# Diagonal blocks copied on chip instead of loaded twice, six loads moved to another queue, and two groups of tiles shifted by 64 bytes

## The chip, the core and the metric

The kernel runs on one core of a Trainium2 chip. A core has five engines that run side by side, each with its own queue of instructions that it works off in order: TensorE (PE, matrix products, with its weight loads listed apart as PEld), VectorE (DVE), ScalarE (ACT), GpSimd (POOL) and SyncE (SP), which here only issues transfers. ACT can issue transfers too; its other work then waits while it does. The transfers themselves run on 16 DMA engines. On-chip memory (SBUF) has 128 partitions; matrix products land in PSUM.

The metric is the device time of one execution in microseconds (us), as a median of several runs.

## The reference, cut to what matters

Two layers of a sequence encoder work on 256 positions of 1024 channels in float32. Each layer mixes positions by a retention branch and by a gated delta rule in both directions, merges the two with gates, and then applies a feed-forward block.

```python
for l in range(DEPTH):                       # 2 layers
    h = rmsnorm(x, norm1_g[l])
    (r_q, r_k, r_v, r_g, d_q, d_k, d_v, d_z, d_b, d_a, gate_raw) = split_cols(h @ w_in[l])
    y_ret = ...                              # retention, normed, times silu(r_g)
    od = gated_delta_bidir(dq, dk, dv, beta_f, beta_b, g_f, g_b)
    y_dn = ...                               # od normed, times silu(d_z)
    merged = gates[:, :, 0] * (y_ret @ w_proj_ret[l]) + gates[:, :, 1] * (y_dn @ w_proj_dn[l])
    x = x + merged @ w_out[l]
    h2 = rmsnorm(x, norm2_g[l])
    x = x + jnp.square(jax.nn.relu(h2 @ w_ff1[l])) @ w_ff2[l]
return rmsnorm(x, final_g)
```

The delta rule works in chunks of 128 positions. In each chunk, head and direction it solves a unit triangular system:

```python
a_mat = bc[..., :, None] * jnp.einsum('bhnid,bhnjd->bhnij', kc, kc) * dec_strict
lhs = a_mat + jnp.eye(CHUNK, dtype=jnp.float32)
sol = lax.linalg.triangular_solve(lhs, rhs, left_side=True, lower=True, unit_diagonal=True)
```

There are 8 heads, 2 chunks and 2 directions, which is 32 triangles of 128 x 128 in each layer.

## The kernel before

**Dense products.** Every weight matrix is read from HBM once. `tok_chunk` (L185) and `chan_pair` (L203) load raw tiles of 512 KB through SP's queue (L191, L209; tile names wraw and wrawc, three buffers), ACT makes a rounded high part (L181, whi), DVE the low remainder (L182, wlo), and PE adds three products of high and low parts (L198 to L200, or L216 to L218). The accumulators are named after their use: pcd are the delta inputs, padz and pcga the gates, pcpr and pcpd the two projections, pawo the output projection, pcf and paf the two feed-forward products. In `chan_pair` a row of weights is the stationary operand and 256 positions stream past; in `tok_chunk` the activations are stationary and 512 columns of weights stream.

**The triangular systems.** `delta_kk` (L435) forms the matrices, and `delta_solve` (L469) inverts all their 32 x 32 diagonal blocks at once on DVE into X (L482 to L488), copies the transposed inverses to XT (L490) and stores both to HBM as xd and xtd (L492, L493). `delta_levels` (L496) then builds the inverse of each 128 x 128 matrix from these blocks, for two halves of four heads (hf 0 and 1). Three tiles take the blocks from HBM, in pieces of 32 partitions x 8 matrices x 32 columns (32 KB each):

- dd (L514, L515), 8 loads: plane 0 and plane 1 hold the diagonal blocks of the direction b % 2, and of the other direction, as the products ps_y (L527) and ps_mt (L544) stream them;
- D64 (L520, named D in the profile), 4 loads: diagonal blocks in the left or right half of 64 columns;
- DTt (L522, named DT), 8 loads: the diagonal blocks of the transposed inverses; the rest of each tile is zeroed first by GpSimd (L517).

That is 20 loads for each half, 40 in a layer, all issued by SP. Four of the eight DTt blocks and two of the four D64 blocks of a half hold the same numbers as a block of dd on the same partitions. The steps that follow are small products in float32: ps_y, then W is rewritten (L530 on DVE, L532 on ACT), then ps_m (L537) fills D64 (L539), ps_mt fills the off-diagonal DT blocks (L547, L549), and two more products with 64 columns (L558, L568) finish the inverse. ps_y and ps_mt stream 32 columns past 128 x 128 weights.

**Order.** The two halves are generators that `drive` steps in turn. Which instruction an engine gets next is fixed before the run by a scheduler with a simulated clock: of those whose inputs it expects to be ready, the one that stands earlier in the program is put first, and loads and conversions of raw weights are moved 45 places ahead (WPRI). So dense work that stands later in the program fills PE's time while the small products wait. The gate product pcga and then the retention projection pcpr are the dense work behind `delta_levels`; the program's text has the small loads before the loads of pcpr's weights, and SP's queue holds them in that order. The DTt tiles of the second half share memory with X and XT, so their zeroing waits for the stores xd and xtd to end.

**Memory.** Tiles come from pools, one slot size for all users of a tag, slots one after the other. mTh and mTl, the high and low part of the merged branches and the stationary operands of pawo, use the two slots of tag E, which earlier hold the decay matrices E (L324). fh and fl, eight tiles each, are the stationary operands of paf; their pool lies at the start of a region that in layer 1 begins with the small pool fin (L826).

Of the kernel before, what the change touches and what calls it, by code (L numbers as in the profile page):

```python
# [9 lines left out]
F32R = mybir.dt.float32r  # L10
# [4 lines left out]
P = 128  # L15
D = 1024
S = 256
# [18 lines left out]
def tile_trunk(ctx, tc, x, norm1_g, w_in, conv_w, a_log, dt_bias, ret_gn_g, dn_norm_g,  # L36
               w_proj_ret, w_proj_dn, w_out, norm2_g, w_ff1, w_ff2, final_g, consts, out):
    nc = tc.nc
    DQ = nc.sync
    V, A, G, T = nc.vector, nc.scalar, nc.gpsimd, nc.tensor  # L40

    def pool(name, bufs, space=None, c=ctx):
        kw = {} if space is None else {"space": space}
        return c.enter_context(tc.tile_pool(name=name, bufs=bufs, **kw))
# [181 lines left out]
    for l in range(DEPTH):  # L226
        mctx = ctx.enter_context(ExitStack())
        mx = pool(f"mx{l}", 1, None, mctx)
        dl = pool(f"dl{l}", 1, None, mctx)
# [201 lines left out]
        blk = [slice(32 * b, 32 * b + 32) for b in range(4)]  # L431
# [64 lines left out]
        def delta_levels(hf, q):  # L496

            Av = q["Av"]
            D64 = D64h[hf]
            xv, xtv = (t[64 * hf:64 * hf + 64].rearrange("(d u b) (a e) -> d b a u e", d=2, b=4, e=32)  # L500
                       for t in (sc["xd"], sc["xtd"]))
            Dv = (xtv, xv)
            DTv = (xv, xtv)
            W = sc["W"][hf]
            dd = dl.tile([P, 2, 8, 32], F32, tag="dd", name="dd", bufs=2)
            if hf == 0:
                DTt = [hp.tile([P, 8, P], F32, tag=f"x{d}", name=f"DT{d}") for d in range(2)]
            else:
                DTt = [dl.tile([P, 8, P], F32, tag="GX"[d], name=f"DT{d}") for d in range(2)]
            G.memset(D64, 0.0)  # L510
            for b in range(4):

                d = b % 2
                DQ.dma_start(dd[blk[b], 0], Dv[d][d, b])  # L514
                DQ.dma_start(dd[blk[b], 1], DTv[1 - d][1 - d, b])  # L515
            for d in range(2):
                G.memset(DTt[d], 0.0)  # L517
                for e in range(2):
                    b = 2 * d + e
                    DQ.dma_start(D64[blk[b], :, 32 * e:32 * e + 32], Dv[d][d, b])  # L520
                for b in range(4):
                    DQ.dma_start(DTt[d][blk[b], :, blk[b]], DTv[d][d, b])  # L522
            yield

            ps = dps.tile([P, 8, 32], F32, tag="dps", name="ps_y")
            for u in range(8):
                T.matmul(ps[:, u, :], lhsT=W[:, u, :], rhs=dd[:, 0, u, :], start=True, stop=True)  # L527
            for d, b, c in PAIRS:
                if d:
                    V.tensor_copy(W[blk[c], :, blk[b]], ps[blk[c]])  # L530
                else:
                    A.activation(W[blk[c], :, blk[b]], ps[blk[c]], AF.Copy)  # L532
            yield
            for d, b, c in ((0, 0, 1), (1, 3, 2)):
                pm = dps.tile([P, 512], F32, tag="dps", name="ps_m")
                for u in range(8):
                    T.matmul(pm[:32, 32 * u:32 * u + 32], lhsT=DTt[d][:, u, blk[c]], rhs=W[:, u, blk[b]],  # L537
                             start=True, stop=True)
                V.tensor_scalar(D64[blk[c], :, 32 * (b % 2):32 * (b % 2) + 32],  # L539
                                pm[:32, :256].rearrange("p (u c) -> p u c", u=8), -1.0, None, ALU.mult)  # L540
            yield
            ps = dps.tile([P, 8, 32], F32, tag="dps", name="ps_mt")
            for u in range(8):
                T.matmul(ps[:, u, :], lhsT=W[:, u, :], rhs=dd[:, 1, u, :], start=True, stop=True)  # L544
            for d, b, c in PAIRS:
                if d:
                    V.tensor_scalar(DTt[d][blk[b], :, blk[c]], ps[blk[b]], -1.0, None, ALU.mult)  # L547
                else:
                    A.activation(DTt[d][blk[b], :, blk[c]], ps[blk[b]], AF.Copy, scale=-1.0)  # L549
            half = (slice(0, 64), slice(64, 128))  # L550
            yield

            Y6 = dl.tile([P, 8, 64], F32, tag="dd", name="Y6", bufs=2)
            for d in range(2):
                ss, oo = half[d], half[1 - d]
                ps = dps.tile([P, 8, 64], F32, tag="dps", name="ps_y6")
                for u in range(8):
                    T.matmul(ps[:64, u, :], lhsT=Av[d][ss, u, oo], rhs=D64[ss, u, :], start=True, stop=True)  # L558
                if d:
                    V.tensor_copy(Y6[oo], ps[:64])  # L560
                else:
                    A.activation(Y6[oo], ps[:64], AF.Copy)
            yield
            for d in range(2):
                ss, oo = half[d], half[1 - d]
                ps = dps.tile([P, 8, 64], F32, tag="dps", name="ps_m6")
                for u in range(8):
                    T.matmul(ps[:64, u, :], lhsT=Y6[oo, u, :], rhs=DTt[d][oo, u, oo], start=True, stop=True)  # L568
                if d:
                    V.tensor_scalar(DTt[d][ss, :, oo], ps[:64], -1.0, None, ALU.mult)  # L570
                else:
                    A.activation(DTt[d][ss, :, oo], ps[:64], AF.Copy, scale=-1.0)
            q.update(DT=DTt)
# [162 lines left out]
        def delta():  # L736
            qs = []
            for hf in range(2):
                q = yield from half_inputs(hf)
                delta_kk(hf, q)  # L740
                qs.append(q)
            delta_solve()
            yield
            drive(*(delta_levels(hf, qs[hf]) for hf in range(2)))
            for hf in range(2):
                yield from half_v(hf, qs[hf])
            yield
            drive(*(delta_out(hf, qs[hf]) for hf in range(2)))
# [28 lines left out]
        def gate(off, dst, nm):  # L777

            for i in range(4):
                ps = chan_pair(wl_[:, off + 256 * i:off + 256 * (i + 1)], hT_hi, hT_lo, nm)  # L780
                for e in range(2):
                    t_ = dst[i // 2][:, 2 * (i % 2) + e, :]
                    A.activation(t_, ps[e], AF.Tanh, scale=0.5)

        mT = [mx.tile([P, 4, S], F32, tag=f"sg{j}", name=f"mT{j}") for j in range(2)]
# [12 lines left out]
               lambda k: gT2[:, 32 + l:33 + l], yTh, yTl, "yd")  # L798
        tB = [dl.tile([P, 4, S], F32, tag=t, name="tB" + t, bufs=2) for t in ("ktok", "kq0")]
        gate(O_GB, tB, "gb")  # L800
        mTh, mTl = (dl.tile([P, 2, 4, S], F32R, tag="E", name="mT" + n, bufs=2) for n in "hl")
        mTh, mTl = ([m[:, j] for j in range(2)] for m in (mTh, mTl))
        for i in range(4):
            ps = chan_pair(w_proj_dn[l][:, 256 * i:256 * (i + 1)], yTh, yTl, "pd")
            for e in range(2):
                k = 2 * (i % 2) + e
# [21 lines left out]
        ff = pool(f"ff{l}", 1, None, fctx)  # L828
# [2 lines left out]
        r2 = rms("2", xh)  # L831
        rr2 = sm.tile([P, NT], F32, tag="rr2", name="rr2")
        V.tensor_tensor(rr2, r2, r2, ALU.mult)
        fh = [ff.tile([P, 4, S], F32R, tag=f"fh{i}", name=f"fh{i}") for i in range(8)]
        fl = [ff.tile([P, 4, S], F32R, tag=f"fl{i}", name=f"fl{i}") for i in range(8)]
        for i in range(16):
            ps = chan_pair(w_ff1[l][:, 256 * i:256 * (i + 1)], hT_hi, hT_lo, "f1")
            for e in range(2):
                k = 2 * i + e
# [20 lines left out]
        if last:  # L860

            r = fin.tile([P, NT], F32, tag="fr", name="fr")
            o = fin.tile([P, NT, D], F32, tag="o", name="o")
# [57 lines left out]
```

## Time and profile before

| | us |
|---|---|
| runs | 1119.09, 1125.75, 1119.31 |
| median of the runs | 1119.31 |
| the profiled execution | 1122.8 |
| its span | 1121.1 |
| mean granted TensorE clock | 0.974 |

The profiled execution ran 3.5 us longer than the median; 1.7 us of its time lie outside its span. The page of the profile gives each engine's busy time and share of the span, and then rows with the span cut in 40 slices of 28 us, each digit a share in tenths. The row PEclk shows the TensorE clock that was granted in a slice. Matmuls are pipelined, so their durations overlap: the pace of a series is read from the distance of their starts. A row of the timeline gives start, duration, engine, line, operation, the tile written and the tiles read, the count of merged instructions, and in brackets the idle time before it and what ended that. SPq and ACTq rows are the issue of a transfer, not its run.

### The profile page before, as it was taken

Reading aid. Unit: us, or ns where it says so; the run is one execution under the profiler, and the core shown is the slowest. Engines: PE = TensorE matmul, PEld = TensorE weight load, DVE = VectorE, ACT = ScalarE, POOL = GpSimd, SP = SyncE. Lnnn points to the kernel's source line nnn. Section 1 sums busy time; section 2 is a strip of 40 time slices with the busy share of each in tenths; the row PEclk is TensorE's granted clock in tenths of the full one; section 3 lists DMA queues with packets and bytes.
Section 4 is the critical chain, followed back from the end, with each engine's and each line's share of the span. In section 5 each row is a group of like instructions: output and inputs, shape, how many; then the busy total and the mean of one; then the engine's idle time right before and its main releaser. Section 6 shows DMA issues by size and latency. Waiting matters only on the chain.

```text
span 1121.1 us, 19644 instructions
## 1 busy us (share of the span) xinstructions
PE 1077.8 (96%) x7564; PEld 998.3 (89%) x7564; DVE 761.1 (68%) x1375; ACT 594.9 (53%) x1030; POOL 217.5 (19%) x237
## 2 busy tenths in 40 slices
PE   6989999999999999999979899999999999999997
PEld 5989888989999899988879888889999999999885
DVE  4879989735676676644469799895465766766453
ACT  5986555523354566533369765454333546665342
POOL 3076210100012043300020952000000111332000
PEclk9999999969999999999999999999699999999999
DMA  6575665553545566556556646656435465665563
GB/s 213 160 202 148 188 189 157 148 138 114 151 129 174 169 202 184 185 187 207 176 166 178 183 149 170 187 151 140 139 108 151 143 203 165 204 188 187 190 190 111
DMA packets 175760, 188.44 MB, mean 168 GB/s; under 512 B 36240, under 2 KB 137010, under 8 KB 175666
## 3 DMA queue, kind: packets, MB, share of 16 engines
q1 hardware_dynamic: 174288, 185.17, 55.5%
q10 hardware_dynamic: 1378, 2.02, 0.5%
q8 instruction: 59, 0.97, 0.4%
q14 instruction: 35, 0.29, 0.1%
HBM read 181.85 MB, written 5.31 MB: 167 GB/s over the span
## 4 chain that ended last, share of the span: by engine, by line
PE 41%; POOL 3%; DVE 3%; SPq 1%; DMA 1%; issue 1%; ACT 1%; POOLq 0%
PE pcf L218 3%; PE pcf L216 3%; PE pcf L217 3%; PE paf L200 3%; PE paf L198 3%; PE paf L199 3%; POOL E L335 3%; PE pcd L216 1%; PE pcd L217 1%; PE pcd L218 1%; DVE wlo L182 1%; PE pcpr L217 1%; PE pcpr L216 1%; PE pcpr L218 1%; PE parg L199 1%; PE pcpd L218 1%
## 5 line engine op out<-in xcount | busy, mean ns | idle before, releaser
L182 DVE TENSOR_TENSOR wlo<-wrawc,whi 128x1024 fp32r<-128x1024 f32 x192 | 238.1, 1241 | 111.9 <-ACT whi L181 110.6
L181 ACT ACTIVATE whi<-wrawc 128x1024 fp32r<-128x1024 f32 x192 | 202.4, 1057 | 141.6 <-PE pcpr L217 22.1
L181 ACT ACTIVATE whi<-wraw 128x1024 fp32r<-128x1024 f32 x128 | 135.6, 1059 | 183.2 <-PE paf L200 91.5
L182 DVE TENSOR_TENSOR wlo<-wraw,whi 128x1024 fp32r<-128x1024 f32 x128 | 156.7, 1227 | 109.1 <-ACT whi L181 109.1
L217 PE MATMUL pcf<-h2l,whi 128*128 128x256 f32 x512 | 142.4, 281 | 0.0
L218 PE MATMUL pcf<-h2h,wlo 128*128 128x256 f32 x512 | 141.6, 281 | 0.0
L216 PE MATMUL pcf<-h2h,whi 128*128 128x256 f32 x512 | 140.8, 282 | 0.0
L216 PE MATMUL pcd<-hTh,whi 128*128 128x256 f32 x384 | 111.3, 294 | 2.4 <-DVE rw L662 2.4
L217 PE MATMUL pcd<-hTl,whi 128*128 128x256 f32 x384 | 109.9, 287 | 0.0
L218 PE MATMUL pcd<-hTh,wlo 128*128 128x256 f32 x384 | 108.5, 288 | 0.0
L199 PE MATMUL paf<-wlo,fh 128*128 128x512 f32 x256 | 100.7, 393 | 0.0
L200 PE MATMUL paf<-whi,fl 128*128 128x512 f32 x256 | 100.7, 393 | 0.0
L217 PEld LDWEIGHTS pcf<-h2l,whi 128*128 128x128 f32 x512 | 98.0, 191 | 0.0
L218 PEld LDWEIGHTS pcf<-h2h,wlo 128*128 128x128 f32 x512 | 95.9, 188 | 0.0
L216 PEld LDWEIGHTS pcf<-h2h,whi 128*128 128x128 f32 x512 | 95.0, 188 | 0.0
L198 PE MATMUL paf<-whi,fh 128*128 128x512 f32 x256 | 90.5, 393 | 0.0
L843 POOL TENSOR_TENSOR fz<-fz 128x256 f32<-128x256 f32 x64 | 68.3, 1068 | 112.0 <-ACT fz L842 94.8
L216 PEld LDWEIGHTS pcd<-hTh,whi 128*128 128x128 f32 x384 | 74.5, 195 | 4.2 <-issue 2.5
L335 POOL TENSOR_SCALAR E<-E,gx 128x128 f32<-128x128 f32 x64 | 58.9, 940 | 95.9 <-DMA E<-rowd 50.1
L217 PEld LDWEIGHTS pcd<-hTl,whi 128*128 128x128 f32 x384 | 74.5, 194 | 0.5
L218 PEld LDWEIGHTS pcd<-hTh,wlo 128*128 128x128 f32 x384 | 73.5, 194 | 0.6 <-DVE wlo L182 0.3
L364 DVE SCALAR_TENSOR_TENSOR cacc<-pcd,cw,cacc 128x255 f32<-128x255 f32 (+1 forms) x144 | 67.3, 477 | 6.2 <-ACT cac L360 5.1
(266 smaller groups left out, 2644.3 us busy)
## 6 DMA issues: line engine op xcount, KB each, us to landing
wrawc<-in_w_in_dram SPq DMA_DIRECT2D x96, 512.0 KB, 3.9
wrawc<-in_w_ff_dram SPq DMA_DIRECT2D x64, 512.0 KB, 3.8
wraw<-in_w_ff_dram SPq DMA_DIRECT2D x64, 512.0 KB, 3.6
wraw<-in_w_in_dram SPq DMA_DIRECT2D x48, 512.0 KB, 3.7
wrawc<-in_w_proj_ret_dram SPq DMA_DIRECT2D x16, 512.0 KB, 3.7
wrawc<-in_w_proj_dn_dram SPq DMA_DIRECT2D x16, 512.0 KB, 3.4
wraw<-in_w_out_dram SPq DMA_DIRECT2D x16, 512.0 KB, 3.8
E<-rowd SPq DMA_DIRECT2D x16, 256.0 KB, 5.6
```

The costliest lines, as they stand in the source:

```text
L181: A.activation(hv, raw, AF.Copy)
L182: V.tensor_tensor(lv, raw, hv.bitcast(F32), ALU.subtract)
L198: T.matmul(ps[t], lhsT=a, rhs=wh[:, kk, :], start=k == 0, stop=False)
L199: T.matmul(ps[t], lhsT=a, rhs=wl[:, kk, :], start=False, stop=False)
L200: T.matmul(ps[t], lhsT=b, rhs=wh[:, kk, :], start=False, stop=k == nk - 1)
L216: T.matmul(ps[i], lhsT=wh[:, kk, c], rhs=a, start=k == 0, stop=False)
L217: T.matmul(ps[i], lhsT=wh[:, kk, c], rhs=b, start=False, stop=False)
L218: T.matmul(ps[i], lhsT=wl[:, kk, c], rhs=a, start=False, stop=k == KT - 1)
L335: G.tensor_scalar(E[:, c, h, :], E[:, c, h, :], gc[:, c, u:u + 1], 0.0, ALU.subtract, ALU.min)
L364: V.scalar_tensor_tensor(a[:, o], ps[i][:, q], wk(k), a[:, o], ALU.mult, ALU.add)
L843: G.tensor_tensor(z2, z, z, ALU.mult)
```

## The change

It touches four places.

1. In `delta_levels`, both DTt tiles are zeroed ahead of the loads.
2. Of the eight DTt blocks, the four with d != b % 2 are copied by GpSimd from plane 1 of dd; of the four D64 blocks, the two with d == e are copied from plane 0. These 12 copies in a layer are of 32 partitions x 256 numbers and take the place of 12 loads.
3. The other four DTt loads and two D64 loads of a half are issued by SP in the first half and by ACT in the second (`q_`). The eight dd loads of each half stay with SP. In a layer SP now issues 22 small loads and ACT 6.
4. mTh now starts 64 bytes into its slot; mTl starts at the beginning of its slot, and as each slot of the tag has become 64 bytes longer, the second slot begins 64 bytes later. In layer 0 the tile fh0 begins 64 bytes into its slot, which is longer by as much, so that all tiles of that pool behind it are shifted too. In layer 1 that pool is as before.

```diff
             G.memset(D64, 0.0)
+            for d in range(2):
+                G.memset(DTt[d], 0.0)
+            q_ = (DQ, nc.scalar)[hf]
             for b in range(4):
 
                 d = b % 2
                 DQ.dma_start(dd[blk[b], 0], Dv[d][d, b])
                 DQ.dma_start(dd[blk[b], 1], DTv[1 - d][1 - d, b])
-            for d in range(2):
-                G.memset(DTt[d], 0.0)
-                for e in range(2):
-                    b = 2 * d + e
-                    DQ.dma_start(D64[blk[b], :, 32 * e:32 * e + 32], Dv[d][d, b])
-                for b in range(4):
-                    DQ.dma_start(DTt[d][blk[b], :, blk[b]], DTv[d][d, b])
+
+            for d, b in ((0, 1), (1, 2), (0, 0), (0, 2), (1, 1), (1, 3), (0, 3), (1, 0)):
+                if d != b % 2:
+                    G.tensor_copy(DTt[d][blk[b], :, blk[b]], dd[blk[b], 1])
+                else:
+                    q_.dma_start(DTt[d][blk[b], :, blk[b]], DTv[d][d, b])
+            for b in range(4):
+                d, e = b // 2, b % 2
+                to = D64[blk[b], :, 32 * e:32 * e + 32]
+                if d == e:
+                    G.tensor_copy(to, dd[blk[b], 0])
+                else:
+                    q_.dma_start(to, Dv[d][d, b])
             yield
...
-        mTh, mTl = (dl.tile([P, 2, 4, S], F32R, tag="E", name="mT" + n, bufs=2) for n in "hl")
+        mTh, mTl = (dl.tile([P, 16 + 8 * S], F32R, tag="E", name="mT" + n, bufs=2)[:, o:o + 8 * S]
+                    .rearrange("p (j k s) -> p j k s", j=2, k=4) for n, o in (("h", 16), ("l", 0)))
...
-        fh = [ff.tile([P, 4, S], F32R, tag=f"fh{i}", name=f"fh{i}") for i in range(8)]
+
+        lead = 16 if l == 0 else 0
+        fh = [ff.tile([P, lead * (i == 0) + 4 * S], F32R, tag=f"fh{i}", name=f"fh{i}")[:, lead * (i == 0):]
+              .rearrange("p (k s) -> p k s", k=4) for i in range(8)]
```

## The prediction

> **What bounds the kernel now.** I read the page's busy shares first, then its clock row, then TensorE's waits, then a table of windows laid on the half-clock stretches.
>
> ```profile
> span 1121.1 us, 19644 instructions
> PE 1077.8 (96%) x7564; PEld 998.3 (89%) x7564; DVE 761.1 (68%) x1375; ACT 594.9 (53%) x1030; POOL 217.5 (19%) x237
> PEclk9999999969999999999999999999699999999999
> PE ps_y L527 <- DMA dd<-xd: 3.2, 2, 2.2
> ```
>
> TensorE (PE) is busy 96% of the span, so only two things can pay: time in which it stands, and time in which it runs slowly. The wait that this change touches is small, 3.2 us in two pieces (one in each layer). What follows it is larger:
>
> ```profile
> 225.47:228.88 3.41, 1.24 (x12) 1.07 (x10) 0.00 (x0) 0.38 (x1) 0.00 (x0) 1.00 0.42 67
> 228.88:245.95 17.07, 16.54 (x124) 16.18 (x124) 7.78 (x13) 5.30 (x9) 0.00 (x0) 0.50 0.63 177
> 587.28:590.69 3.41, 1.90 (x17) 1.70 (x16) 1.79 (x7) 2.57 (x5) 0.00 (x0) 1.00 0.82 253
> 655.55:658.96 3.41, 2.10 (x15) 1.92 (x16) 3.28 (x9) 1.06 (x1) 0.93 (x2) 1.00 0.45 147
> 778.43:781.84 3.41, 2.33 (x26) 2.12 (x25) 0.00 (x0) 0.50 (x2) 0.00 (x0) 1.00 0.41 66
> 781.84:805.73 23.89, 22.83 (x174) 21.85 (x172) 9.69 (x15) 6.83 (x11) 0.00 (x0) 0.50 0.48 143
> ```
>
> Columns: stretch, length, busy time of PE, weight loads, DVE, ACT and POOL, then granted clock, DMA share, GB/s. Right behind the stall the granted clock is 0.50 for 17.07 us in layer 0 and for 23.89 us in layer 1. A stretch with 1.90 us or 2.10 us of PE work (587.28, 655.55) keeps the clock at 1.00 beyond it; the one at 778.43 holds more, 2.33 us, and loses it. The difference is the kind of work, seen in PE's timeline:
>
> ```profile
> 226.05 0.28 PE L218 MATMUL pcga<-hTh,wlo 128*128 128x256 f32 x1
> 228.50 3.24 PE L527 MATMUL ps_y<-dd,W 128*128 128x32 f32 x16 [2.17 <-DMA dd<-xd]
> 236.13 7.04 PE L544 MATMUL ps_mt<-dd,W 128*128 128x32 f32 x32
> 243.77 0.41 PE L217 MATMUL pcpr<-yrl,whi 128*128 128x256 f32 x1
> 243.98 0.41 PE L218 MATMUL pcpr<-yrh,wlo 128*128 128x256 f32 x1
> 246.29 0.28 PE L217 MATMUL pcpr<-yrl,whi 128*128 128x256 f32 x1
> 246.40 0.28 PE L218 MATMUL pcpr<-yrh,wlo 128*128 128x256 f32 x1
> 779.74 1.94 PE L527 MATMUL ps_y<-dd,W 128*128 128x32 f32 x16 [1.08 <-DMA dd<-xd]
> 781.62 0.93 PE L537 MATMUL ps_m<-W,DT 128*32 128x32 f32 x16
> 783.05 2.12 PE L537 MATMUL ps_m<-W,DT 128*32 128x32 f32 x32 [0.51 <-DVE D L539]
> 786.66 7.04 PE L544 MATMUL ps_mt<-dd,W 128*128 128x32 f32 x32
> 793.51 0.56 PE L216 MATMUL pcpr<-yrh,whi 128*128 128x256 f32 x1
> 797.20 3.31 PE L558 MATMUL ps_y<-D,A 64*64 64x64 f32 x32
> 808.92 1.90 PE L568 MATMUL ps_m<-DT,Y 64*64 64x64 f32 x32
> ```
>
> When the dense gate work (pcga) ends at 226.33, PE has only thin matmuls, 32 columns wide, and no dense work to mix in. Dense work (pcpr) begins at 242.98 in layer 0 and at 793.51 in layer 1. At half clock pcpr matmuls start 0.21 us apart (243.77, 243.98), at full clock 0.11 to 0.12 (246.29, 246.40; I use 0.117). Why no dense work: the pcpr weights stand behind the small loads on SP's queue.
>
> ```profile
> 211.94 0.33 SPq L514 DMA_DIRECT2D dd<-xd  x1
> 220.27 3.16 SPq L522 DMA_DIRECT2D DT<-xtd  x4
> 226.92 0.45 SPq L515 DMA_DIRECT2D dd<-xd  x1
> 233.39 23.41 SPq L209 DMA_DIRECT2D wrawc<-in_w_proj_ret_dram  x8
> 764.22 0.33 SPq L514 DMA_DIRECT2D dd<-xd  x1
> 778.19 0.45 SPq L515 DMA_DIRECT2D dd<-xd  x1
> 784.65 26.74 SPq L209 DMA_DIRECT2D wrawc<-in_w_proj_ret_dram  x8
> ```
>
> Forty small loads fill the queue from 211.94 to 233.39 (21.45 us, 0.54 each) and from 764.22 to 784.65 (20.43 us).
>
> **The change, part by part.** *Loads removed or moved.* Of 20 loads in each half, 6 become copies; in the second half 6 more go to ACT. SP keeps 8+6 and 8, which is 22 of 40. At the same price each SP needs 11.8 us in layer 0 and 11.2 us in layer 1: the first pcpr weight is issued near 223.7 (9.7 us earlier) and near 775.5 (9.2 us earlier). The last dd load, whose landing ended PE's wait 1.6 us after its issue (226.92 to 228.50), would land by about 225 and 777, before pcga ends. So the waits of 2.17 and 1.08 us go. What is late next is PE's own thin chain and its evacuations (the 0.5 us idle before ps_m).
>
> *The stretch at full clock.* One thin group of 16 ps_y takes 1.88 us (779.74 to 781.62). I price ps_mt, of the same shape, equally, though no row shows it at full clock: 3.76 us for both halves. Four ps_m groups at 0.93 are 3.72, three gaps of 0.51 are 1.53. Sum 10.9 us, against 16.65 in layer 0 (226.33 to 242.98) and 14.84 in layer 1 (778.67 to 793.51): 5.7 and 3.9 us saved. Behind it, 14 pcpr matmuls of layer 0 at 0.21 and not 0.117 cost 1.3 us; in layer 1 33 of them cost 3.2 us, and two ps_y groups about 2.0 (3.31 against 1.90, the second half as much). If the clock never falls: 7.0 + 9.1 = 16.1 us. That is one end.
>
> *If the clock falls all the same.* Thin work alone may suffice: at 778.43, 2.33 us of mostly thin work lost it. Then each ps_mt pair costs 7.04 again (3.3 more per layer) and the dense work behind pays on average what it pays now ((1.3+5.2)/2 = 3.3): 16.1 - 6.6 - 6.6 = 2.9 us. That is the other end. I take the middle, 9.5 us, as one layer of two kept at full clock. Reasons for both: the first half's DT loads now end at 223.43 (220.27 + 3.16); with 14 loads at 0.54 they end near 219.5, four microseconds earlier, so its ps_m and ps_mt can fall among pcga; but thin work has priority over dense, so it still bunches.
>
> The Trainium skill, page "TensorE: Matmul & The Clock Gate", section on the HAM clock gate, says the half rate follows an idle window of about 3.4 us. The trace disagrees: stalls of 2.17 and 1.08 us were enough with thin work beside them. By the page's rule alone the clock would stay up once the wait is gone, and the sum would be 16.1 and not 9.5.
>
> *The copies.* Twelve a layer on GpSimd, of the shape that the kernel copies already:
>
> ```profile
> L460 POOL COPY W<-A x16: 386/398/1423, 116.4 to 696.8; 32x256 f32<-32x256 f32 x16
> 215.95 0.96 POOL L517 MEMSET DT<- 128x1024 f32 x1 [2.96 <-DMA dd<-xd]
> 212.48 1.06 ACT L181 ACTIVATE whi<-wrawc 128x1024 fp32r<-128x1024 f32 x1 [0.91 <-PE pcga L217]
> ```
>
> At 0.4 us they are 4.8 us a layer, at the slowest row 17. POOL has nothing else between 212 and 247 but the two memsets. I take 0.4 and cost them at nothing; a copy starts when its dd block has landed, so a half's six end 2.4 us behind the last, while ps_y and its evacuation run (about 3 us). Without that cover they cost up to 2.4 us a half.
>
> *ACT's queue.* Six issues at SP's 0.45 to 0.54 us are about 3 us of ACT's in-order queue per layer. Behind them stand weight conversions (L181), PSUM evacuations of pcga and those of ps_y. ACT is busy 5.30 us of 17.07 in the stretch above, which hides them if they are issued after the DT memset, which ends at 216.91; I take nothing. The moved memsets cost nothing where they stand.
>
> *Tiles moved by 64 bytes.* fh is the stationary operand of the second feed-forward product:
>
> ```profile
> L198 PE MATMUL paf<-whi,fh x128: 397/397/400, 471.9 to 560.8; 128*128 128x512 f32 x128
> L198 PE MATMUL paf<-whi,fh x128: 388/389/401, 1026.2 to 1112.6; 128*128 128x512 f32 x128
> L198 PE MATMUL pawo<-whi,mTh x32: 388/397/400, 357.6 to 379.7; 128*128 128x512 f32 x32
> L198 PE MATMUL pawo<-whi,mTh x32: 388/397/400, 911.9 to 934.0; 128*128 128x512 f32 x32
> 400.00:556.00 156.00, 156.00 (x973) 140.05 (x972) 86.86 (x87) 76.98 (x113) 28.86 (x27) 1.00 0.60 190
> ```
>
> Same code, same clock, other addresses: 88.9 us for 381 steps in layer 0 (0.2333), 86.4 in layer 1 (0.2268). Only layer 0 is moved; if that brings it to layer 1's pace it saves 384 x 0.0066 = 2.5 us. The mT products show the slow 397 ns in both layers: 96 x 0.0066 x 2 = 1.3 us. Ends: 0 if the address is not the cause, 3.8; a loss of as much cannot be excluded. I take 3.8, because PE is without a gap there (156.00 us busy of 156.00), so each step saved is time saved. The page "SBUF: State Buffer", section "SBUF: two separate sides" of the Trainium skill, says PE never waits on anyone for SBUF and names no such address effect; by it this term is 0 and the sum 9.5.
>
> **Sum.** 9.5 + 3.8 = 13.3 us. The profiled execution took 1122.8 us, which gives 1109.5; the median of the runs is 1119.31, 3.5 lower, which gives 1106.0.
>
> **The rivals.** (a) *The clock stays at 1.00 in both layers*, because dense pcga and pcpr now lie between the thin groups: 16.1 + 3.8 = 19.9, 1099.4; with the ps_m gaps filled too, some 3 less. For it: after 805.73 thin groups of 1.9 us alternate with dense work at full clock (808.92). (b) *It falls again in both*: 2.9 + 3.8 = 6.7, 1112.6. For it: the row at 778.43. (c) *The change doesn't do what it says*: the schedule places other work so that neither the loads nor the addresses count: 1116 to 1119. Against it: the DMA wait row names dd. (d) *The addresses change nothing*, and the two paces come from something else that differs between the layers: 9.5 alone, 1109.8. Against it: 381 steps keep one pace in each layer, under the same code. (e) *Slower: ACT blocks.* If ACT reaches its six loads before the memset ends (216.91), it stands from 213.5 to 216.9, then issues for 3 us; conversions for pcga come 6.4 us late. Two converted weight tiles ahead cover 24 matmuls of 0.117 each, 5.6 us; so from a block of about 5.6 us PE stands. With nothing of the 16.1 gained, 0.8 us standing and a further 3.41 us at half clock (1.5 us) per layer, plus a loss of 3.8 at the moved tiles: 4.6 + 3.8 = 8.4, 1127.7; with the tiles gaining, 1120.
>
> **Chances.** Forecast (one layer at full clock) 0.30; (a) 0.26; (b) 0.20; (c) 0.08; (d) 0.10; (e) 0.06. The forecast's own range is 1102 to 1110. Faster by over 1% (about what a measurement of this kernel can tell from no change) means under 1108.1: all of (a), most of the forecast and a little of (b) and (d), 0.54. Over 1130.5 needs more than (e): 0.05. Within 1%: 0.41. The range 1097 to 1117 takes in the forecast, (a), (b) and (d) and half of (c), and leaves out somewhat under 0.2.
>
> **What would show it.** Right: 22 small loads on SP's queue per layer, pcpr weights issued some 9 us earlier, no wait of ps_y on dd, less than 17.07 and 23.89 us at clock 0.50, paf in layer 0 at 389 ns, mT products too. Wrong: ps_y still waiting, now on a copy or on ACT; ACT idle before L181 while its queue issues; half-clock stretches of the old length; paf at 397.

## The result and the profile after

The changed kernel takes 1107.47 us (median of 4 runs, 1105.80 to 1109.83), the kernel before on the same chip 1119.69 us. The ratio is 0.988 with a 95% interval of 0.9841 to 0.9919. Timed once more later, beside the experiments, it took 1104.24 us (6 runs) against 1121.04 us: 0.9852, 0.9809 to 0.9894. So the change is worth 12.2 to 16.8 us by medians; 13.3 us were predicted. The profiled execution of the changed kernel took 1105.8 us, 17.0 us less than the one of before (1122.8).

The page of the changed kernel, its span, TensorE's share, the clock row, and from the waits those that touch the delta stage (total, times, longest):

```profile
span 1104.1 us, 19634 instructions
PE 1060.6 (96%) x7564; PEld 983.0 (89%) x7564; DVE 766.9 (69%) x1375; ACT 594.3 (54%) x1030; POOL 235.0 (21%) x261
PEclk9999999999999999999999999999999999999999
PE pcpr L216 <- ACT whi L181: 1.6, 2, 1.0
PE ps_y L536 <- DMA dd<-xtd: 0.7, 1, 0.7
PE ps_y L536 <- DMA dd<-xd: 0.6, 1, 0.6
```

TensorE's busy share is as before, 96%, but its busy time fell from 1077.8 to 1060.6 us: the gain is not idle time removed (43.3 us of the span before, 43.5 after), it is the same matmuls run faster. The two sixes of the old clock row, behind the small loads of each layer, are gone. The wait of ps_y on dd shrank from 3.2 to 1.3 us, and a new one of 1.6 us stands behind it: pcpr on the conversion of its weights.

SP's queue of the changed kernel (start, time to issue), the ends of the small loads in both layers and the weights behind them:

```profile
211.38 0.33 SPq L517 DMA_DIRECT2D dd<-xd  x1
217.90 1.71 SPq L524 DMA_DIRECT2D DT<-xtd  x2
224.59 0.45 SPq L518 DMA_DIRECT2D dd<-xd  x1
225.14 13.41 SPq L209 DMA_DIRECT2D wrawc<-in_w_proj_ret_dram  x7
...
757.16 0.33 SPq L517 DMA_DIRECT2D dd<-xd  x1
770.29 19.74 SPq L209 DMA_DIRECT2D wrawc<-in_w_proj_ret_dram  x8
```

The small loads now hold the queue for 13.76 us (211.38 to 225.14) and 13.13 us, where it was 21.45 and 20.43 us.

TensorE's timeline of the changed kernel shows what those seven to eight microseconds did:

```profile
226.73 1.87 PE L536 MATMUL ps_y<-dd,W 128*128 128x32 f32 x16
229.79 0.39 PE L216 MATMUL pcpr<-yrh,whi 128*128 128x256 f32 x1 [0.57 <-ACT whi L181]
237.44 3.65 PE L553 MATMUL ps_mt<-dd,W 128*128 128x32 f32 x32
...
771.45 1.94 PE L536 MATMUL ps_y<-dd,W 128*128 128x32 f32 x16 [0.56 <-DMA dd<-xd]
775.05 0.52 PE L216 MATMUL pcpr<-yrh,whi 128*128 128x256 f32 x1 [1.03 <-ACT whi L181]
784.15 3.65 PE L553 MATMUL ps_mt<-dd,W 128*128 128x32 f32 x32
```

Dense pcpr matmuls begin at 229.79 and 775.05, between the thin groups (242.98 and 793.51 before, after all those of 32 columns). The 32 ps_mt matmuls take 3.65 us, where they took 7.04. Windows over the thin stretch of layer 0, and over two neighbouring windows in layer 1 (columns as in the prediction's table):

```profile
226.73:241.09 14.36, 13.79 (x162) 13.30 (x161) 8.49 (x13) 7.18 (x10) 0.17 (x1) 1.00 0.76 252
771.73:775.14 3.41, 2.38 (x32) 2.22 (x31) 0.52 (x2) 1.17 (x2) 0.38 (x1) 1.00 1.06 340
775.14:778.56 3.42, 3.42 (x26) 3.13 (x27) 3.14 (x5) 2.75 (x4) 0.00 (x0) 0.50 0.61 199
```

In layer 0 the clock is 1.00 throughout (0.50 for 17.07 us before). In layer 1 it is 0.50 for one window of 3.41 us (23.89 us before): the window ahead of it, 771.73 to 775.14, holds thin matmuls, the wait of 1.03 us, and almost nothing dense (the wait of 0.56 us ends just ahead of it).

The two engines that took over work, POOL's last copies and ACT's queue:

```profile
226.15 0.40 POOL L529 COPY D<-dd 32x256 f32<-32x256 f32 x1
226.50 0.40 POOL L522 COPY DT<-dd 32x256 f32<-32x256 f32 x1
```

```profile
217.53 0.46 ACTq L531 DMA_DIRECT2D D<-xtd  x1
218.04 0.84 ACT L174 ACTIVATE yrh<-pstyr,gT 128x256 fp32r<-128x256 f32 x2 [4.25 <-DMA DT<-xtd]
763.06 0.84 ACT L174 ACTIVATE yrh<-pstyr,gT 128x256 fp32r<-128x256 f32 x2 [3.52 <-POOL DT L522]
```

The copies end at 226.90, while the second half's ps_y runs. ACT stood behind its loads for 4.25 and 3.52 us.

The moved tiles, first products of paf (layer 0) and pawo (both layers):

```profile
L198 PE MATMUL paf<-whi,fh x128: 389/389/401, 464.5 to 550.9; 128*128 128x512 f32 x128
L198 PE MATMUL pawo<-whi,mTh x32: 389/389/401, 350.7 to 372.3; 128*128 128x512 f32 x32
L198 PE MATMUL pawo<-whi,mTh x32: 389/389/401, 895.4 to 916.9; 128*128 128x512 f32 x32
```

paf takes 86.4 us in layer 0, as it does in layer 1, and not 88.9; pawo 21.6 and 21.5 us and not 22.1.

**Where the time went in the profiled pair.** A yardstick that leaves the moved tiles out is the time from the issue of the store of X to the first pawo matmul. For layer 0 it is made of this row and the pawo row above (350.7 - 207.37 = 143.3):

```profile
207.37 0.34 SPq L492 DMA_DIRECT2D xd<-X  x1
```

Before, it was 149.8 us in layer 0 and 151.8 in layer 1; after, 143.3 and 143.1. That is 6.5 + 8.7 = 15.2 us from the delta stages. The tiles give 2.5 + 0.5 + 0.6 = 3.6. The sum, 18.8, is 1.8 above the difference of the spans (17.0). It is made of 0.4 us gained ahead of the first store of X (207.37 against 207.76) and 2.1 us lost between the layers: paf of layer 0 ends 9.9 us earlier than before, but the store of X in layer 1 is issued only 7.8 us earlier (752.31 against 760.13). There the changed kernel has a window at half clock:

```profile
580.58:584.00 3.42, 3.42 (x18) 3.42 (x17) 3.42 (x13) 2.18 (x5) 0.00 (x0) 0.50 0.16 58
```

Ahead of it TensorE stood for a conversion:

```profile
580.11 0.44 PE L385 MATMUL ps_kt<-ident,kq 128*128 128x128 f32 x2 [2.26 <-ACT kq L383]
```

The kernel before kept the clock at the same work some 10 us later (the prediction's row of 587.28), with a stand of 1.51 us. Such short windows come and go between executions, and each costs about half its length (an estimate: matmuls at half rate start 0.21 us apart and not 0.117). The same kernel profiled a second time ("the change again" below) has none here and none in either delta stage, though TensorE ran nearly the same rows in layer 1: ps_y, ps_m, a stand of 1.05 us for the conversion, then pcpr at 774.91. Its clock changed at 633.81 (the change nearest ahead of these rows), and multiples of 3.41 us from there cut the rows at 773.76, so that each of the two windows holds dense work:

```profile
770.35:773.76 3.41, 3.41 (x41) 3.25 (x40) 0.00 (x0) 0.67 (x2) 1.19 (x3) 1.00 0.79 239
773.76:777.17 3.41, 2.36 (x32) 2.09 (x29) 2.65 (x5) 2.87 (x4) 0.00 (x0) 1.00 0.74 241
```

In the first execution the window from 771.73 held the thin rows and the stand alone. So where the boundary falls seems to decide in such a case; that is read from two executions and was not tested.

### The profile page after: what moved, and what is told of

It reads as the page before. It is cut to its first block, busy times and chain, and to the rows that moved or that the text cites. A ratio compares the mean times of both kernels' runs of the same rounds, so it can differ in the third digit from the quotient of the medians.

```text
span 1104.1 us, 19634 instructions
## 1 busy us (share of the span) xinstructions
PE 1060.6 (96%) x7564; PEld 983.0 (89%) x7564; DVE 766.9 (69%) x1375; ACT 594.3 (54%) x1030; POOL 235.0 (21%) x261
## 5 line engine op out<-in xcount | busy, mean ns | idle before, releaser
L217 PE MATMUL pcf<-h2l,whi 128*128 128x256 f32 x512 | 142.4, 281 | 0.0
```

The costliest lines, as they stand in the source:

```text
L217: T.matmul(ps[i], lhsT=wh[:, kk, c], rhs=b, start=False, stop=False)
```

## The experiments

The theory was: the gain is dense work that reaches TensorE sooner and keeps its clock up, plus a pace of the matmuls that depends on the address of the stationary tile. Rivals: the wait on the loads is itself what lowers the clock; ACT's share of the loads is the gain, or a loss; the pace comes from something other than addresses.

The table holds, for each kernel, how long the small loads (and whatever else was put in front) held SP's queue ahead of pcpr's weights, and the yardstick above, both in layers 0 and 1, from one profiled execution; then the median with the ratio to the kernel before, timed on the same chip.

| kernel | queue held, us | store of X to pawo, us | median us, ratio |
|---|---|---|---|
| before | 21.45, 20.43 | 149.8, 151.8 | |
| tiles alone | 20.80, 21.10 | 149.7, 149.1 | 1113.41, 0.995 (0.9921 to 0.9979) |
| ACT's loads alone | 17.64, 16.52 | 145.2, 147.1 | 1113.01, 0.9953 (0.9931 to 0.9976) |
| copies alone, rest on SP | 15.39, 15.81 | 143.2, 143.9 | 1105.10, 0.9876 (0.9834 to 0.9917) |
| copies and ACT, no tiles | 13.93, 13.30 | 145.1, 144.1 | 1107.38, 0.990 (0.9864 to 0.9937) |
| the change | 13.76, 13.13 | 143.3, 143.1 | 1107.47, 0.988 |
| the change again | 12.56, 12.35 | 142.1, 141.0 | 1104.24, 0.9852 (0.9809 to 0.9894) |
| copies and tiles, rest on SP | 15.00, 15.28 | 143.8, 144.3 | 1100.56, 0.9817 (0.9779 to 0.9855) |
| the same again | 15.27, 15.04 | 142.4, 143.6 | 1105.71, 0.9852 (0.9817 to 0.9888) |
| 14 loads on ACT | 10.43, 8.52 | 144.6, 142.1 | 1103.18, 0.9846 (0.9809 to 0.9884) |
| the change, weights late | 24.12, 21.90 | 159.8, 147.4 | 1119.74, 0.9988 (0.9949 to 1.0027) |

The two middle columns come from one execution each and scatter by some 3 us: layer 1 has 151.8 before and 149.1 with the tiles alone, whose loads are the same. The mean granted clock is on record for every execution. It was 0.966 to 0.982 in the 45 executions of the kernel before that were timed with the experiments, 0.969 to 0.980 with the tiles alone and 0.968 to 0.974 with the weights late; 0.983 to 0.987 with ACT's loads alone; and 0.984 to 0.992 in all other kernels with the copies. So the higher clock comes with the loads and not with the tiles, and in every execution.

The first four experiments ran beside a kernel before of 1119.17 us, the next four beside 1121.71 us, the last two beside 1121.04 us.

**Tiles alone.** The kernel before with part 4 of the change and nothing else.

```diff
-        mTh, mTl = (dl.tile([P, 2, 4, S], F32R, tag="E", name="mT" + n, bufs=2) for n in "hl")
+        mTh, mTl = (dl.tile([P, 16 + 8 * S], ...)[:, o:o + 8 * S]... for n, o in (("h", 16), ("l", 0)))
-        fh = [ff.tile([P, 4, S], F32R, tag=f"fh{i}", name=f"fh{i}") for i in range(8)]
+        fh = [ff.tile([P, lead * (i == 0) + 4 * S], ...)[:, lead * (i == 0):]... for i in range(8)]
```

> The kernel before with the two moved groups of tiles alone. Theory (the address of the stationary tile sets the pace, and the loads set the clock): paf in layer 0 takes 389 ns a matmul and not 397, pawo 389 in both layers, the half-clock stretches behind the small loads stay near 17 and 24 us; 3.8 us faster, a ratio of 0.9966. Rival (the pace is a state that a long series of matmuls falls into by chance, whatever the address): paf or pawo at 397 somewhere, ratio 1.000 within 0.002.

Measured: 0.995, or 5.6 us with an interval of 2.4 to 8.8. Its windows over the half-clock stretches, and its paf in layer 0:

```profile
231.20:248.27 17.07, 16.18 (x126) 15.54 (x124) 7.86 (x13) 5.31 (x9) 0.00 (x0) 0.50 0.66 199
780.80:794.45 13.65, 12.66 (x81) 12.30 (x82) 6.49 (x10) 4.56 (x7) 0.00 (x0) 0.50 0.72 220
...
L198 PE MATMUL paf<-whi,fh x128: 389/389/392, 469.6 to 556.0; 128*128 128x512 f32 x128
```

The long half-clock stretches stay (17.07 and 13.65 us), paf takes 86.4 us. The tiles have an effect of their own, and rival (d) of the prediction falls. Of the tiles that paf reads, only fh and fl have moved; the converted weights lie in another pool.

**Copies and ACT without the tiles.** The changed kernel with the old forms of mTh, mTl and fh (the diff above, reversed).

> The change without the moved tiles: 6 copies a half, 6 loads of the second half by ACT. Theory: 12.2 less 3.8, which is 8.4 us faster than before, a ratio of 0.9925; half-clock stretches behind the small loads at most 3.4 us each; paf in layer 0 at 397 again. Rival (chance state of the pace): paf in layer 0 at 389 all the same, ratio 0.989.

Measured: 0.990. paf of layer 0 is back at its old pace, 88.9 us:

```profile
L198 PE MATMUL paf<-whi,fh x128: 397/397/400, 465.9 to 554.8; 128*128 128x512 f32 x128
```

The two parts are separable, and the pace of paf follows the tile and nothing in the delta stage. Most of the change's gain is in the loads. The clock did not stay up as long as expected: behind the small loads of layer 1 it is at half for 6.83 us (778.68 to 785.50), not for 3.4 at most.

**Copies alone.** As the one before, with the remaining 28 loads all on SP.

```diff
-            q_ = (DQ, nc.scalar)[hf]
+            q_ = DQ
```

> The copies alone: no load goes by ACT, no tile is moved; SP issues 28 small loads a layer. Theory (what counts is when the dense weights reach the queue): pcpr's first weights are issued some 3 us later than with 22 loads and some 6 us earlier than with 40, so part of the gain stays, 3 to 7 us faster than before, ratio 0.994 to 0.997. Rival (the ACT part is worth nothing, since all transfers share the DMA engines): as the change without the moved tiles, 0.9925.

Measured: 0.9876, better than I had expected of it. The queue is held two microseconds longer than with ACT's help, and the stage is no longer for that. TensorE's waits on dd, and pawo in layer 0:

```profile
PE ps_y L536 <- DMA dd<-xd: 2.2, 2, 1.3
PE ps_y L536 <- DMA dd<-xtd: 0.5, 1, 0.5
L198 PE MATMUL pawo<-whi,mTh x32: 388/388/393, 352.9 to 374.6; 128*128 128x512 f32 x32
```

ps_y still waits for dd for 2.7 us, against 3.2 before the change, and the gain is there all the same: it did not come from a shorter wait. And pawo takes 21.7 us (21.8 in layer 1) and not 22.1, although no tile was moved here. So the address of mT is not all that sets the pace of pawo.

**ACT's loads alone.** The kernel before with the second half's twelve DT and D loads on ACT, and no copies.

```diff
+            q_ = (DQ, nc.scalar)[hf]
...
-                    DQ.dma_start(D64[blk[b], :, 32 * e:32 * e + 32], Dv[d][d, b])
-                    DQ.dma_start(DTt[d][blk[b], :, blk[b]], DTv[d][d, b])
+                q_.dma_start(DTt[d][blk[b], :, blk[b]], DTv[d][d, b])
+                q_.dma_start(to, Dv[d][d, b])
```

> No copies and no moved tiles: all 20 blocks of a half are loaded, the 12 DT and D64 loads of the second half by ACT; SP issues 28 small loads a layer. Theory (issue order on SP counts): like the copies alone, ratio 0.994 to 0.997, with ACT standing some 6 us longer a layer. Rival (ACT blocked by its loads holds up the conversions): ratio 1.000 or above, with PE waiting for whi of pcga.

Measured: 0.9953. SP has as many loads as in the experiment before, 28, but here the gain is 5.3 us and not 13.9. TensorE's waits show a part of the price:

```profile
PE pcga L216 <- ACT whi L181: 2.4, 2, 1.2
PE pcga L218 <- DVE wlo L182: 1.0, 2, 0.5
```

This is the rival (e) of the prediction in small: with twelve loads ACT converts pcga's weights too late, and TensorE stands 3.4 us. The waits of ps_y on dd are down to 0.9 us here, against 2.7 with the copies alone, and the gain is less than half of theirs.

**The weights made late again.** The changed kernel with 18 loads into an unused tile on SP's queue, between the small loads and pcpr's weights. The dd loads keep their early place, so the wait on them stays short, and only the dense work is late. This tells the wait from the lack of dense work.

```diff
+            if hf:
+                for r in range(18):
+                    b = r % 4
+                    DQ.dma_start(scr[blk[b]], xv[0, b])
```

> The changed kernel with 18 more small loads on SP in each layer, behind the second half's dd loads and ahead of pcpr's weights; they fill a scratch tile that nobody reads (the output is the reference's). The dd blocks land as early as in the changed kernel, the dense weights as late as before the change. Theory (the thin matmuls lose the clock when no dense work lies between them): no wait of ps_y on dd over 1 us, but half clock for 7 to 24 us behind the small loads in each layer and 5 to 12 us lost against the changed kernel, ratio to before 0.993 to 0.999. Rival (an idle PE loses the clock, and the removed wait was its cause): the clock stays up, at most 3 us lost, ratio 0.988 to 0.991.

Measured: 0.9988, the gain gone, that of the tiles with it. The weights come even later than before the change, by 2.7 us of queue in layer 0 and 1.5 in layer 1; the stage is 10 us longer than before in layer 0 and 4.4 us shorter in layer 1 (147.4 against 151.8). SP's queue, then TensorE's timeline, then windows:

```profile
225.82 0.46 SPq L519 DMA_DIRECT2D dd<-xd  x1
226.32 10.10 SPq L536 DMA_DIRECT2D scr<-xd  x18
236.46 37.22 SPq L210 DMA_DIRECT2D wrawc<-in_w_proj_ret_dram  x8
```

```profile
229.32 1.87 PE L541 MATMUL ps_y<-dd,W 128*128 128x32 f32 x16
231.12 0.69 PE L551 MATMUL ps_m<-W,DT 128*32 128x32 f32 x16
232.41 0.66 PE L551 MATMUL ps_m<-W,DT 128*32 128x32 f32 x16 [0.60 <-DVE D L553]
233.29 1.82 PE L551 MATMUL ps_m<-W,DT 128*32 128x32 f32 x32 [0.21 <-DVE W L544]
235.03 7.04 PE L558 MATMUL ps_mt<-dd,W 128*128 128x32 f32 x32
```

```profile
229.99:233.40 3.41, 2.60 (x47) 2.39 (x47) 1.47 (x4) 0.75 (x2) 0.00 (x0) 1.00 0.42 66
233.40:267.53 34.13, 34.13 (x236) 32.01 (x235) 11.23 (x17) 7.98 (x12) 0.00 (x0) 0.50 0.35 103
789.80:806.87 17.07, 17.07 (x126) 16.67 (x127) 6.99 (x11) 5.62 (x9) 0.00 (x0) 0.50 0.51 145
```

The first half's ps_y, at 221.76, had waited 1.06 us (the trace names a copy into DT as what ended it), and the clock was at half for 3.41 us behind it; from 226.56 it is at 1.00 again. From there on no thin group waits for a load: the longest gap is 0.60 us, TensorE is busy 2.60 of the 3.41 us before 233.40, and the clock falls for 34.13 us, twice as long as before the change. In layer 1, too, it falls behind a window with 2.63 us of work and gaps of 0.60 us at most. What lowers the clock here is thin work without dense work in between; the wait on the loads was no condition for it. (A stand can lower it too, as the 2.26 us ahead of 580.58 in the changed kernel showed.)

**Copies and tiles, all loads on SP**, and **the dd loads of the second half on ACT too** (q_ in place of DQ in their two lines, so that SP and ACT issue 14 each).

> The whole change but for the ACT queue: copies and moved tiles, all 28 remaining small loads by SP. Theory A (ACT's part costs as much as it gives, since ACT stands while its loads wait, and the moved tiles add their 3.8 us to the copies): 3 us faster than the copies alone, ratio 0.984 to 0.986, below the changed kernel. Theory B (fewer loads on SP are always better): slower than the changed kernel, ratio 0.990 or more.

> The changed kernel with the second half's eight dd loads moved to ACT as well: SP issues 14 small loads a layer, ACT 14. Theory B (SP's queue is the limit): pcpr's weights are issued 4 us earlier still, 2 to 4 us faster than the changed kernel, ratio 0.985. Theory A (ACT stands longer): ACT idle before its loads grows over the 4.25 us of the changed kernel, conversions come late, PE waits for whi; ratio 0.990 to 1.000.

Measured: 0.9817 and 0.9846. In the second kernel ACT stands longer than in any other, and TensorE gets a wait on DVE's rewriting of W:

```profile
225.37 0.77 ACT L541 ACTIVATE W<-ps_y 32x256 f32<-32x256 f32 x2 [10.51 <-DMA dd<-xd]
PE ps_m L546 <- DVE W L539: 2.4, 2, 1.2
```

The 10.51 us did no more harm than that, and pcpr's weights, though three to five microseconds earlier again, brought nothing more. The first kernel's 1100.56 us was the lowest median of all and suggested that ACT's loads cost time. That needed a comparison side by side:

> The changed kernel itself, beside the version that keeps all 28 remaining loads on SP. If ACT's six issues cost time (theory, from the two separate results 0.988 and 0.982), it gives 0.986 to 0.990 of before, 4 to 8 us above the other kernel, with ACT standing some 4 us behind its loads in each layer. If the difference of those results was only scatter, both land within 3 us of each other.

> Copies and shifted tiles, no load on ACT, timed again beside the changed kernel. Theory (ACT's queue is a loss, SP's 28 loads leave the clock up all the same): 0.980 to 0.984 of before, half-clock stretches of 3.41 us at most in each layer, no long stand of ACT. Rival (scatter): 0.985 to 0.989, as the changed kernel.

Measured: 1104.24 us for the change and 1105.71 us for the version without ACT, both 0.9852. The difference of the earlier results was scatter; moving six loads to ACT is neither a gain nor a loss once the copies are there. No version was shown to beat the change.

**Other distances for the tiles.** The changed kernel with fh0 at 128 bytes in layer 0 and 64 in layer 1, and mTh at its slot's start; one run.

```diff
-... for n, o in (("h", 16), ("l", 0)))
+... for n, o in (("h", 0), ("l", 0)))
-        lead = 16 if l == 0 else 0
+        lead = 32 if l == 0 else 16
```

> The changed kernel with other offsets: fh starts 128 bytes into its slot in layer 0 and 64 bytes in layer 1 (0 after the change), mTh at 0 and mTl at 0, whose slot begins 64 bytes later. Theory (what counts is the address in 64 byte steps, even or odd): paf steps of 0.233 us in both layers, layer 1 slower than ever; pawo mixed, the products that read mTh slow and those that read mTl fast. Rival (the pace is chance, or only the distance to some other tile matters): paf 0.227 in one layer at least.

Measured: 1113.89 us in a single run. paf in layer 0 and in layer 1:

```profile
L198 PE MATMUL paf<-whi,fh x128: 393/398/398, 466.2 to 555.1; 128*128 128x512 f32 x128
L198 PE MATMUL paf<-whi,fh x128: 392/396/398, 1014.8 to 1103.7; 128*128 128x512 f32 x128
```

Both layers now take 88.9 us. Layer 1, which steps at 0.2268 us before and after the change, loses it when its tiles move by 64 bytes, and layer 0 loses it at a further 64. But the pace is of another kind here: steps of 230 to 236 ns mixed, where the kernel before had 233 throughout. So the address sets the pace of paf, but not by a plain rule of odd and even multiples of 64 bytes. pawo did not come out as expected either: its products that read mTh (medians 394 and 393 ns) are no slower than those that read mTl (392).

## Why the prediction was right, and where it was not

1106.0 was predicted, 1107.47 and 1104.24 were measured. By its steps:

**The queue.** Right in kind: SP keeps 22 small loads and the weights follow early. The price was too low: 13.76 us for 22 loads is 0.63 each (0.60 in layer 1) and not 0.54. The first weights came 8.3 us earlier in layer 0, not 9.7; in layer 1 the queue is held 7.3 us less, not 9.2. The table shows that this did not matter: with the queue held anywhere from 8.5 to 15.8 us the stage takes 141.0 to 145.1 us.

**The waits of ps_y.** Said to go; 1.3 of 3.2 us stayed, now at other places. What I named as late next, TensorE's own thin chain and its evacuations, was not; it was ACT's conversion of the first pcpr tile (1.6 us).

**The stretch at full clock.** The assumed price of ps_mt, 3.76 us for 32, was shown to be 3.65; a group of 16 ps_m takes 0.69 and not 0.93. The prediction's ends were 16.1 us (the clock never falls) and 2.9 (it falls in both layers), and it took the middle, 9.5, as one layer warm. This is the term that was mis-sized. Both layers stayed warm but for one window, and the stage gave 15.2 us in the profiled pair: 6.5 in layer 0 against 7.0 at the warm end, 8.7 in layer 1 against 9.1. The second execution of the changed kernel, with no half-clock window in either stage, stood at 142.1 and 141.0, which is 7.7 + 10.8 = 18.5 us. The mechanism of rival (a) is what happened, and not one layer warm and one cold. The prediction had the reason in hand (dense pcga and pcpr between the thin groups) and gave as much weight to the fear that thin work, which goes first, would bunch whatever the queue did. Rival (b) would have shown long half-clock stretches in both layers, and rival (c) the old order of TensorE's work; neither is in the trace.

**Why the total came out near all the same.** The prediction took the median to lie 3.5 us below the profiled execution both times. The profiled run of before lay 3.1 us above its median, that of after 1.7 us below, so the pair shows 17.0 us where the medians show 12.2. That 4.8 us nearly cancels the 15.2 - 9.5 = 5.7 us missing from the stage. The second timing, 16.8 us, is nearer to the pair. So it is partly luck that 1106.0 lies so near to 1107.47.

**The clock.** The Trainium skill, page "TensorE: Matmul & The Clock Gate", section on the HAM clock gate, gives an idle window of about 3.4 us as what brings the half rate back. The late-weights run disagrees: 2.60 us busy in the 3.41 us window with no gap above 0.60 us, and then 34.13 us at 0.50. The same section says that the gate goes by how busy TensorE has been in a window of that length; the stretches at half clock here, 3.41, 6.83, 13.65, 17.07, 23.89 and 34.13 us, all multiples of 3.41, agree with that part.

**The copies.** Right: 0.40 us each, covered by ps_y, cost nothing. They are the part that carries the gain: alone they give 0.9876, ACT's loads alone 0.9953 (both with the earlier zeroing, which was not tried by itself).

**ACT's queue.** "I take nothing" held for six loads: 4.25 and 3.52 us of standing, under the 5.6 us that rival (e) named as its point (two converted tiles of 24 matmuls each, at 0.117). With twelve loads (ACT's loads alone) the rival's mechanism is there, with 3.4 us of waits.

**The tiles.** 3.8 us predicted, 3.6 in the profiled pair (2.5 for paf, 1.1 for pawo), 2.4 to 8.8 by the timing of the tiles alone. For paf the address is shown as the cause: its step in layer 0 is 0.233 us in the four profiled executions with the old tiles and 0.227 in the seven with the shift. For the 1.1 us of pawo it is not, since pawo was faster with the copies alone as well. The Trainium skill, page "SBUF — State Buffer", section "SBUF: two separate sides", says that TensorE never waits on anyone for SBUF and names no effect of an address; the trace shows one of 0.0066 us in each 128x512 step.

**What stays open.** The parts do not add up exactly: copies alone (13.9 us) and tiles alone (5.6) would make 19.5, and the change gives 12.2 to 16.8; the intervals are some 4 us wide on either side, so this may be scatter alone. Why the pace of paf has three patterns by address is not known, nor what else sets that of pawo. How much dense work is enough to hold the clock was only bracketed, and where the boundaries of the 3.41 us windows fall may shift the limit: seen lost at the window of 771.73, seen kept through 226.73 to 241.09, and at the stand for kq seen kept at 1.51 us and lost at 2.26 us.

## What to carry to other kernels

Look at the granted clock behind a short wait before pricing the wait: here 3.2 us of waiting stood in front of 41 us at half rate, and what cured it was dense work between the thin matmuls, not a shorter wait. Count the transfers ahead of the next large load in an in-order queue, and remove them (a copy on an idle engine) rather than spread them; once the large load is early enough, making it earlier still brings nothing. Time two versions side by side before one is called better: 1100.56 and 1105.71 us are the same kernel.

## What the runs showed of the hardware

- TensorE's clock fell to half without a long stand: products of 32 columns, 2.60 us busy of 3.41 and no gap above 0.60 us, were enough. It then stayed at half for 34.13 us, with TensorE busy throughout on thin and some dense products.
- A shift of the stationary tiles by 64 bytes took the 128x512 step of paf in layer 0 from 0.2333 to 0.2268 us. A further 64 bytes there, or 64 in layer 1, gave a mix of 0.230 to 0.236 us with the old mean.
- A load of 32 KB in pieces of 32 partitions mostly took 0.45 us of the issuing queue, 0.54 with what lay between, so forty of them held the 512 KB loads behind them back for 20 to 21 us.
